# One gate group of each pair of FFN blocks in seven products of weight and token sums

## The chip, the cores and the metric

The kernel runs on one core of a Trainium2 chip. The core has a matrix engine (PE, with its weight loads listed as PEld), a vector engine (DVE), a scalar engine (ACT), a general engine (POOL) and a queue engine that issues DMAs (SP). Each works through its own list of instructions in order and waits for others by semaphores. Matmuls write to PSUM, eight banks of 128 x 512 floats; everything else lives in SBUF. The metric is the device time of one execution in microseconds (us); lower is better.

## The reference, cut to what matters

The program is one layer of a diffusion backbone: modulated attention over 256 latent tokens and 256 context tokens, then a modulated SwiGLU feed-forward part (FFN). The change lies in the FFN alone:

```python
D_MODEL = 2048
SEQ = 256
FFN_HIDDEN = -(-8 * D_MODEL // 768) * 256    # 5632

def swiglu(u, w_gate, w_up, w_down):
    return (jax.nn.silu(u @ w_gate) * (u @ w_up)) @ w_down

x = layer_norm(DN_ALPHA * x + g2 * swiglu(modulate(x, sh2, sc2), w_gate[layer], w_up[layer], w_down[layer]),
               ln2_g[layer], ln2_b[layer])
```

All of it is in float32, batch 1, depth 1.

## The kernel before, in words

**Numbers and splits.** PE multiplies in a reduced format (fp32r). So each operand is split in a high half (ACT casts it, L329) and a low half (DVE subtracts the high half from the original, L330), and one product of 128 tokens, 128 features and 512 columns is three matmuls: high by high, high token by low weight, low token by high weight (`mm3`, L338 to L341). The tokens' halves are u2h and u2l, 16 feature tiles of 128 by 256 tokens. Weights come as raw tiles of 4 feature tiles by 512 columns (1 MB, `load_raw`, L309), four raw buffers in all, and are split in two pieces of 128 x 1024 each (`split_raw`), with four buffers for high and four for low pieces. A buffer of a piece is given back when PE has done its last matmul on it.

**Blocks and groups.** The 5632 columns of gate and up are 11 blocks of 512. The 2048 features are four groups of 4 feature tiles (g = 0 to 3). A group of one block is 4 feature tiles x 2 token tiles x 3 = 24 matmuls, 12 on each piece. Because the modulation of the later features is known late, blocks 0 to 9 run in two halves: first group 0 (blocks 0 to 2) or groups 0 and 1 (blocks 3 to 9) of gate and up, whose sums are copied from PSUM to SBUF tiles named spill; later, when all features are there, the other groups. The first of these halves is the list `first_half`; between its steps stand sums for the modulation (adav), and near its end `z_part` transposes, scales and splits the last feature tiles. Block 10 runs whole.

**The second half** is the loop at L1646. For each block it runs gate's groups into two PSUM banks (one for each token tile), then up's into two others, and adds the spilled first half to each (`activate`: L1501 for gate, L1502 for up, on DVE). ACT takes Silu of gate (L1504), DVE multiplies (L1505) and transposes in 32 x 32 squares (L1515). The squares go to DRAM by eight small DMAs ("puts", L1520) and come back by two larger ones ("gets", L1525); ACT and DVE then split the result in halves hTh and hTl (`place`, L335 and L336) for the down projection. `turn()` counts the groups and lets puts, gets and places of a block follow some groups after it. Blocks 5 to 8 also carry `residual_base`, sixteen DVE instructions in all that prepare the residual in xt with LayerNorm rows loaded to a buffer called lgb.

**The order.** An earlier part of the program is placed by a planner of the kernel itself, which the change does not touch. In the FFN the instructions are written in the loops' order, and the framework's scheduler sets each engine's list from dependences, buffers and an estimate of durations, so a step can move ahead of its place in the code. What each engine then runs is fixed, in order.

## Time and profile before

| | |
|---|---|
| median of three runs | 1133.19 us (1132.01 to 1138.03) |
| the profiled execution's own time | 1132.56 us |
| its span, first to last instruction | 1130.8 us |
| mean granted clock of PE | 0.996 |
| casts of weights to high halves, L329 | 258 of 1055 ns |
| low halves of weights, L330 | 258 of 1221 ns |
| matmuls on u2h and u2l, L339 to L341 | 3 x 704 |

Durations that follow come from this one execution. In the list of groups a line's mean is the time of one instruction from its start to its end; instructions of one engine can overlap a little at their ends, and matmuls a lot, so what one costs in a row of them is read from the distance between starts.

### The profile page before, as it was taken

To read this page: it belongs to the slowest core of one execution; us is meant where nothing else is said; L and a number is where in the kernel's file an instruction comes from. 1 tells how busy PE (TensorE), PEld (TensorE's weight loads), DVE (VectorE), ACT (ScalarE), POOL (GpSimd) and SP (SyncE) were. 2 spreads that over 40 slices of the span, in tenths; PEclk is the share of its full clock that TensorE was granted. 3 is DMA by queue.
4 is the path that set the end of the run, shared out by engine and by line. 5 is a ranking of instruction groups with operands and counts; after the bars stand their busy time and mean duration, and the time that the engine had idled before them with its cause. 6 is when DMAs were issued, how large, how long until landed. Compare 5 with 4: busy or idle time off the path is not lost.

```text
span 1130.8 us, 14062 instructions
## 1 busy us (share of the span) xinstructions
PE 1109.5 (98%) x5255; PEld 891.3 (79%) x5255; DVE 844.1 (75%) x1070; ACT 550.8 (49%) x795; POOL 38.7 (3%) x82
## 2 busy tenths in 40 slices
PE   8999999999999999999999999999999999999996
PEld 6766688777887687888888888888888888888884
DVE  5763589999999798777777566776766787686576
ACT  3341554878684265444464444444444344343442
POOL 1000030110100000010000000000000000000000
PEclk9999999999999999999999999999999999999998
DMA  9999999778999768999876776777677898887541
GB/s 308 395 399 371 394 364 357 257 240 280 340 347 372 267 261 315 330 320 314 301 234 214 244 233 223 233 242 257 214 263 242 273 367 305 312 300 252 200 148 74
DMA packets 178317, 321.26 MB, mean 284 GB/s; under 512 B 8732, under 2 KB 43196, under 8 KB 175943
## 3 DMA queue, kind: packets, MB, share of 16 engines
q1 hardware_dynamic: 177528, 320.03, 81.3%
q8 instruction: 41, 0.67, 0.2%
q10 hardware_dynamic: 720, 0.33, 0.1%
q14 instruction: 28, 0.23, 0.1%
HBM read 304.07 MB, written 16.25 MB: 283 GB/s over the span
## 4 chain that ended last, share of the span: by engine, by line
PE 91%; DMA 3%; DVE 2%; ACT 2%; SPq 1%; issue 0%; POOL 0%; ACTq 0%; DVEq 0%; POOLq 0%
PE acc L339 27%; PE acc L340 27%; PE acc L341 27%; PE wk L1079 2%; PE wk L652 2%; DMA raw<-in_w_in_dram 1%; DVE lo L330 1%; PE wk L339 1%; PE wk L753 1%; PE wk L341 1%; PE wk L340 1%; SPq L567 1%; DMA raw<-in_w_ada_dram 1%; DMA raw<-in_w_gate_dram 0%; ACT hi L329 0%; DVE adav L464 0%
## 5 line engine op out<-in xcount | busy, mean ns | idle before, releaser
L330 DVE TENSOR_TENSOR lo<-raw,hi 128x1024 fp32r<-128x1024 f32 x258 | 312.3, 1221 | 165.3 <-ACT hi L329 162.9
L329 ACT CAST hi<-raw 128x1024 fp32r<-128x1024 f32 x258 | 271.1, 1055 | 322.7 <-PE acc L341 296.5
L339 PE MATMUL acc<-hi,u2h 128*128 128x512 f32 x704 | 274.6, 390 | 1.5 <-ACT u2h L1591 1.5
L340 PE MATMUL acc<-lo,u2h 128*128 128x512 f32 x704 | 274.0, 389 | 0.7 <-DVE lo L330 0.7
L341 PE MATMUL acc<-hi,u2l 128*128 128x512 f32 x704 | 274.1, 389 | 0.0
L339 PEld LDWEIGHTS acc<-hi,u2h 128*128 128x128 f32 x704 | 132.1, 188 | 29.6 <-ACT u2h L1591 2.4
L340 PEld LDWEIGHTS acc<-lo,u2h 128*128 128x128 f32 x704 | 132.2, 188 | 28.2 <-DVE lo L330 1.1
L341 PEld LDWEIGHTS acc<-hi,u2l 128*128 128x128 f32 x704 | 132.1, 188 | 28.1 <-DVE u2l L1592 0.6
L601 ACT CAST hi<-raw 128x1024 fp32r<-128x1024 f32 (+1 forms) x86 | 87.5, 1030 | 112.6 <-DMA raw<-in_w_in_dram 63.4
L339 PE MATMUL acc<-hi,hTh 128*128 128x512 f32 x344 | 133.8, 389 | 0.4 <-ACT acc L1742 0.4
L340 PE MATMUL acc<-lo,hTh 128*128 128x512 f32 x344 | 133.9, 389 | 0.0
L341 PE MATMUL acc<-hi,hTl 128*128 128x512 f32 x344 | 133.8, 389 | 0.0
L464 DVE SCALAR_TENSOR_TENSOR adav<-raw,cs,adav 128x512 f32<-128x512 f32 (+1 forms) x128 | 121.3, 948 | 9.2 <-DMA raw<-in_w_ada_dram 7.2
L604 DVE TENSOR_TENSOR lo<-raw,hi 128x1024 fp32r<-128x1024 f32 (+1 forms) x86 | 101.3, 1194 | 13.3 <-ACT hi L601 12.5
L339 PE MATMUL acc<-hi,uh 128*128 128x512 f32 x256 | 103.7, 405 | 2.3 <-ACT qacc L835 1.1
L340 PE MATMUL acc<-lo,uh 128*128 128x512 f32 x256 | 100.3, 392 | 0.5 <-DVE lo L604 0.5
L341 PE MATMUL acc<-hi,ul 128*128 128x512 f32 x256 | 100.1, 391 | 0.4 <-DVE ul L782 0.4
L339 PEld LDWEIGHTS acc<-hi,hTh 128*128 128x128 f32 x344 | 64.6, 188 | 14.2 <-ACT acc L1742 0.8
L340 PEld LDWEIGHTS acc<-lo,hTh 128*128 128x128 f32 x344 | 64.6, 188 | 13.6 <-DVE lo L330 0.2
L341 PEld LDWEIGHTS acc<-hi,hTl 128*128 128x128 f32 x344 | 64.6, 188 | 13.4
L339 PEld LDWEIGHTS acc<-hi,uh 128*128 128x128 f32 x256 | 48.1, 188 | 20.0 <-issue 5.6
L341 PEld LDWEIGHTS acc<-hi,ul 128*128 128x128 f32 x256 | 48.1, 188 | 11.1 <-DVE ul L782 0.7
(224 smaller groups left out, 1142.8 us busy)
## 6 DMA issues: line engine op xcount, KB each, us to landing
raw<-in_w_ada_dram SPq DMA_DIRECT2D x70, 1024.0 KB, 8.0
raw<-in_w_gate_dram SPq DMA_DIRECT2D x44, 1024.0 KB, 5.5
raw<-in_w_up_dram SPq DMA_DIRECT2D x44, 1024.0 KB, 5.6
raw<-in_w_down_dram SPq DMA_DIRECT2D x44, 1024.0 KB, 5.4
raw<-in_w_ada_dram SPq DMA_DIRECT2D x48, 512.0 KB, 5.9
raw<-in_w_in_dram SPq DMA_DIRECT2D x18, 1024.0 KB
raw<-in_w_out_dram SPq DMA_DIRECT2D x16, 1024.0 KB, 5.1
pd<-hx SPq DMA_DIRECT2D x64, 128.0 KB, 5.0
```

The costliest lines, as they stand in the source:

```text
L329: nc.scalar.copy(hi[:, :n], raw[:, s : s + n])
L330: nc.vector.tensor_tensor(lo[:, :n], raw[:, s : s + n], hi[:, :n].bitcast(F32), op=ALU.subtract)
L339: nc.tensor.matmul(ps, lhsT=xh, rhs=w[0], start=first, stop=False, skip_group_check=seeded)
L340: nc.tensor.matmul(ps, lhsT=xh, rhs=w[1], start=False, stop=False, skip_group_check=seeded)
L341: nc.tensor.matmul(ps, lhsT=xl, rhs=w[0], start=False, stop=last, skip_group_check=seeded)
L464: nc.vector.scalar_tensor_tensor(a[:, c : c + piece], raw[:, f : f + piece], cs[:, 4 * (g * (G4 * NB // w) + j) + 2, None], a[:, c : c + p ...
L567: nc.sync.dma_start(room.t, w[k0 * P : (k0 + 1) * P, c0 : c0 + width])
L601: nc.scalar.copy(hl.hi[:, :n], raw.t[:, s : s + n])
L604: nc.vector.tensor_tensor(hl.lo[:, :n], raw.t[:, s : s + n], hl.hi[:, :n].bitcast(F32), op=ALU.subtract)
L652: nc.tensor.matmul(bank.t[32 * j : 32 * j + 32, :width], lhsT=cs[:, 4 * k + 2 - 2 * i : 4 * k + 34 - 2 * i], rhs=raw.t[:, c * width : (c + ...
L753: nc.tensor.transpose(ps.t[:, (j * 2 + t) * P : (j * 2 + t + 1) * P], src, ident)
L1079: nc.tensor.matmul(o_ps.t[:, : 2 * P].rearrange("p (g q) -> p g q", q=32), lhsT=v, rhs=pv[:, k], start=k == 0, stop=k == 3)
```

## The change

For blocks 0 to 9, taken in pairs, the gate group g = 2 (feature tiles 8 to 11) of both blocks is no longer computed as 8 products of 128 tokens x 256 features x 512 columns but as 7, by Winograd's form of Strassen's scheme. The two token tiles by two feature halves make a 2 x 2 matrix, and two feature halves by two blocks another. `token_forms` makes the sums of tokens once, from an unsplit copy (ufs, in the buffer lgb), and splits them (fh, fl). `folded` makes four sums of raw weights in place, in the two raw tiles r1 and r2 of the pair, and runs the seven products, called here by their numbers in the code: 11, 1, 2, 12, 3, 4, 22. Each is 2 feature tiles x 3 = 6 matmuls on one piece. Partial results move between PSUM banks by three ACT copies a pair (L1534, L1542, L1550); the result of product 1 is added by DVE to the spill of the pair's second block (L1545).

Between the products stand up's groups of the two blocks: the order of a late pair is 11, a group of up, 1, a group of up, 2, 12, a group of up, 3, 4, a group of up, 22, then the other gate group of the first block and of the second. So both gate halves of a pair end behind each other, and up is done before them. From block 2 on, up's banks begin with its spilled first half, copied there by ACT (L1724), and ACT copies the finished sums back (L1730); DVE's adds for up remain in the first pair alone. Multiply and transposes of a block are now steps that follow at the next turns. The first-half step of block 3 is put ahead of z_part(4).

```diff
@@ -48,6 +48,7 @@
+FOLD_K = 8
@@ -1463,13 +1464,14 @@
-    def z_part(kk):
+    def z_part(kk, uf=None):
         ps = wk_bank()
...
-        uf = pb.tile([P, 2, SEQ], F32, tag="t2k", name="uf2", bufs=4)
+        if uf is None:
+            uf = pb.tile([P, 2, SEQ], F32, tag="t2k", name="uf2", bufs=4)
@@ -1487,22 +1489,74 @@
-    def project(accs, w_, f, g, first, last):
+    def project(accs, w_, f, g, first, last, seeded=False):
         w = load_split(w_, g * 4, f * NB)
         for j in range(4):
             k = g * 4 + j
             for t in range(NT):
-                mm3(accs[t], u2h[:, k, t * P : (t + 1) * P], u2l[:, k, t * P : (t + 1) * P], w[j], k == first, k == last)
-
-    def activate(f, t, gate, up, hh):
-
-        if f < SPLIT_F:
-            sg, su = spills[f][0][:, t, :], spills[f][1][:, t, :]
-            nc.vector.tensor_add(sg, sg, gate)
-            nc.vector.tensor_add(su, su, up)
-            gate, up = sg, su
-        nc.scalar.activation(hh, gate, AF.Silu)
-        nc.vector.tensor_mul(hh, up, hh)
+                mm3(accs[t], u2h[:, k, t * P : (t + 1) * P], u2l[:, k, t * P : (t + 1) * P], w[j],
+                    k == first and not seeded, k == last, seeded)
+    forms = {}
+    def token_forms(v):
+        v1, v2 = v[:, 0:2, :], v[:, 2:4, :]
+        a11, a21, a12, a22 = v1[:, :, :P], v1[:, :, P:], v2[:, :, :P], v2[:, :, P:]
+        tt = nc.vector.tensor_tensor
+        tt(a22, a21, a22, op=ALU.add)
+        tt(a21, a11, a21, op=ALU.subtract)
+        tt(a11, a22, a11, op=ALU.subtract)
+        tt(a12, a12, a11, op=ALU.subtract)
+        for n, (lr, x) in enumerate((((2, 3), v1), ((4, 1), v2))):
+            hi, lo = (pb.tile([P, 2, SEQ], F32R, tag="t2k", name=name, bufs=4) for name in ("fh", "fl"))
+            split(hi, lo, x)
+            for i, m in enumerate(lr):
+                forms[m] = [(hi[:, j, i * P : (i + 1) * P], lo[:, j, i * P : (i + 1) * P]) for j in range(2)]
+        for m, (t, k) in {11: (0, FOLD_K), 12: (0, FOLD_K + 2), 22: (1, FOLD_K + 2)}.items():
+            forms[m] = [tuple(u[:, k + j, t * P : (t + 1) * P] for u in (u2h, u2l)) for j in range(2)]
+    def fold_products(ps, m, piece, first):
+        w = split_raw(piece)
+        for j in range(2):
+            mm3(ps, *forms[m][j], w[j], first and j == 0, j == 1, not first)
+    def folded(w_, f, between):
+        half = 2 * NB
+        r1, r2 = (load_raw(w_, FOLD_K, G4, (f + i) * NB, NB) for i in range(2))
+        b11, b21, b12, b22 = r1[:, :half], r1[:, half:], r2[:, :half], r2[:, half:]
+        a, e = wk_bank(), wk_bank()
+        b, c, d = (acc_bank() for _ in range(3))
+        tt = nc.vector.tensor_tensor
+        fold_products(a, 11, b11, True)
+        nc.scalar.copy(b, a)
+        tt(b11, b12, b11, op=ALU.subtract)
+        between(0)
+        fold_products(e, 1, b11, True)
+        tt(b12, b22, b12, op=ALU.subtract)
+        tt(b11, b22, b11, op=ALU.subtract)
+        between(1)
+        fold_products(b, 2, b11, False)
+        nc.scalar.copy(c, b)
+        for t in range(NT):
+            sg = spills[f + 1][0][:, t, :]
+            tt(sg, sg, e, op=ALU.add)
+        fold_products(a, 12, b21, False)
+        tt(b21, b21, b11, op=ALU.subtract)
+        between(2)
+        fold_products(c, 3, b12, False)
+        nc.scalar.copy(d, c)
+        fold_products(b, 4, b22, False)
+        between(3)
+        fold_products(c, 22, b21, False)
+        return (a, c), (b, d)
+    def gated_half(f, t, gate):
+        hh = spills[f][0][:, t, :]
+        nc.vector.tensor_add(hh, hh, gate)
+        nc.scalar.activation(hh, hh, AF.Silu)
@@ -1538,9 +1592,17 @@
             hh, hx = ([c[:, t, :] for t in range(NT)] for c in spills[f])
         else:
             hh, hx = ([t2k(name) for t in range(NT)] for name in ("hh", "hx"))
-        for t in range(NT):
-            activate(f, t, gu[0][t], gu[1][t], hh[t])
+        def gated(t):
+            if f >= SPLIT_F:
+                nc.scalar.activation(hh[t], gu[0][t], AF.Silu)
+            nc.vector.tensor_mul(hh[t], gu[1][t], hh[t])
             squares(hh[t], hx[t])
+        late = 1 if f < SPLIT_F else 0
+        if not late:
+            for t in range(NT):
+                gated(t)
         hd, hf = {}, {}
         def puts():
@@ -1556,7 +1618,7 @@
             for t in range(NT):
                 place(f, t, hf[t])
-        return [[PUT, puts], [GET, gets], [PLACE, places]]
+        return [[1 + t, lambda t=t: gated(t)] for t in range(NT * late)] + [[2 * late + n, step] for n, step in ((PUT, puts), (GET, gets), (PLACE, places))]
@@ -1626,12 +1688,15 @@
     run(first_half[2:3])
     run(merge(first_half[3 : 2 * ONE_F], scales))
     combine(1)
+    run(first_half[2 * ONE_F : 2 * ONE_F + 1])
     z_part(4)
     z_part(6)
     cutoff = len(first_half) - 2
-    run(merge(first_half[2 * ONE_F : cutoff], side))
-    for kk in range(EARLY_G * 4, KD, 2):
-        z_part(kk)
+    run(merge(first_half[2 * ONE_F + 1 : cutoff], side))
+    ufs = pb.tile([P, 4, SEQ], F32, tag="lgb", name="ufs")
+    for i, kk in enumerate(range(EARLY_G * 4, KD, 2)):
+        z_part(kk, ufs[:, 2 * i : 2 * i + 2, :] if kk < FOLD_K + 4 else None)
+    token_forms(ufs)
     run(first_half[cutoff:])
     flips = []
@@ -1643,9 +1708,47 @@
             flips.remove(e)
             e[1]()
-    for f in range(FFN // NB):
-        if 5 <= f < 9:
-            residual_base(f - 5)
+    for f0 in range(0, SPLIT_F, 2):
+        for f in (f0, f0 + 1):
+            if 5 <= f < 9:
+                residual_base(f - 5)
+        ups = {}
+        def up(i, g):
+            f = f0 + i
+            su = [spills[f][1][:, t, :] for t in range(NT)]
+            if g == groups[f]:
+                ups[i] = [wk_bank() for _ in range(NT)]
+                for t in range(NT):
+                    if f0:
+                        nc.scalar.copy(ups[i][t], su[t])
+            project(ups[i], w_up, f, g, groups[f] * 4, KD - 1, f0 > 0)
+            turn()
+            if g == ng - 1:
+                for t in range(NT):
+                    if f0:
+                        nc.scalar.copy(su[t], ups[i][t])
+                    else:
+                        nc.vector.tensor_add(su[t], su[t], ups[i][t])
+        def between(n):
+            i, last = divmod(n, 2)
+            gs = range(groups[f0 + i], ng)
+            for g in gs[-1:] if last else gs[:-1]:
+                up(i, g)
+        gates = folded(w_gate, f0, between)
+        for i, f in enumerate((f0, f0 + 1)):
+            for g in range(groups[f], ng):
+                if g * 4 != FOLD_K:
+                    project(gates[i], w_gate, f, g, None, KD - 1, True)
+                    turn()
+            for t in range(NT):
+                gated_half(f, t, gates[i][t])
+            turn()
+            flips += flip_steps(f, (None, [spills[f][1][:, t, :] for t in range(NT)]))
+    for f in range(SPLIT_F, FFN // NB):
         gu = []
         for w_ in (w_gate, w_up):
             accs = [acc_bank() for _ in range(NT)]
```

Three places show how the engines' lists move. A number behind a name tells one tile from another.

DVE, at the end of a gate half late in the stage: before, the adds for gate of block 6 (spill_3712) and what surrounds them.

```order
L330 TENSOR_TENSOR lo_6494<-raw_6487,hi_6493 128x1024
L330 TENSOR_TENSOR lo_6524<-raw_6521,hi_6523 128x1024
L1501 TENSOR_TENSOR spill_3712<-spill_3712,acc_6399 128x512
L1501 TENSOR_TENSOR spill_3712<-spill_3712,acc_6400 128x512
L330 TENSOR_TENSOR lo_6528<-raw_6521,hi_6527 128x1024
L330 TENSOR_TENSOR lo_6579<-raw_6576,hi_6578 128x1024
L330 TENSOR_TENSOR lo_6583<-raw_6576,hi_6582 128x1024
```

DVE, now: the same adds for block 6 (spill_3712) and block 7 (spill_3714); lo_6834 and lo_6892 are low halves for products 11 and 1 of the next pair, whose raw tiles are raw_6824 and raw_6826.

```order
L331 TENSOR_TENSOR lo_6834<-raw_6824,hi_6833 128x1024
L1558 TENSOR_TENSOR spill_3712<-spill_3712,wk_6465 128x512
L1558 TENSOR_TENSOR spill_3712<-spill_3712,acc_6468 128x512
L1535 TENSOR_TENSOR raw_6824<-raw_6826,raw_6824 128x1024
L1599 TENSOR_TENSOR spill_3712<-spill_3713,spill_3712 128x512 x2
L1569 STREAM_TRANSPOSE spill_3713<-spill_3712 128x4x4x32 x2
L331 TENSOR_TENSOR lo_6852<-raw_6849,hi_6851 128x1024
L1558 TENSOR_TENSOR spill_3714<-spill_3714,acc_6467 128x512
L1558 TENSOR_TENSOR spill_3714<-spill_3714,acc_6469 128x512
L331 TENSOR_TENSOR lo_6856<-raw_6849,hi_6855 128x1024
L1599 TENSOR_TENSOR spill_3714<-spill_3715,spill_3714 128x512
L1538 TENSOR_TENSOR raw_6826<-raw_6826 128x1024
```

Before, two adds stand between low halves; now the adds, multiplies and transposes of two blocks and two sums of weights stand between the low halves of two up pieces. The next rows are a transpose, lo_6892, the low half of a piece of up, the third sum of weights, another low half, a multiply, and the low half for product 2.

ACT, where up changes from the first block of a pair to the second (blocks 4 and 5); wk_6120 is a bank of the first, wk_6240 and wk_6241 are the second's. Before, this engine has only casts, Silus and places there.

```order
L330 CAST hi_6229<-raw_6099 128x1024
L336 CAST hTh_6520<-spill_3704 128x4x128
L330 CAST hi_6246<-raw_6244 128x1024
L1730 COPY spill_3709<-wk_6120 128x512
L1724 COPY wk_6240<-spill_3711 128x512
L1730 COPY spill_3709<-wk_6121 128x512
L1724 COPY wk_6241<-spill_3711 128x512
L330 CAST hi_6250<-raw_6244 128x1024
L1542 COPY acc_6106<-acc_6105 128x512
L330 CAST hi_6278<-raw_6101 128x1024
```

Four copies of up, a place that needs a get, and a copy between banks now stand among the casts.

SP, in the pair of blocks 6 and 7: raw_6608 and raw_6669 are the third and fourth load of up, hd is the DRAM buffer of the puts and gets of blocks 4 (spill_3709, spill_3708) and 5.

```order
L310 DMA raw_6540<-in_w_up_dram 128x4x512
L1579 DMA spill_3706<-hd_6435 128x512
L1579 DMA spill_3706<-hd_6440 128x512
L1574 DMA hd_6753<-spill_3709 32x4x128 x4
L1574 DMA hd_6758<-spill_3709 32x4x128 x2
L310 DMA raw_6608<-in_w_up_dram 128x4x512
L1574 DMA hd_6758<-spill_3709 32x4x128 x2
L1579 DMA spill_3708<-hd_6753 128x512
L1574 DMA hd_6805<-spill_3711 32x4x128
L310 DMA raw_6669<-in_w_up_dram 128x4x512
```

Before, in the same place for block 4 (gate loads raw_6441, up loads raw_6487 and raw_6521):

```order
L1520 DMA hd_6475<-spill_3709 32x4x128 x3
L309 DMA raw_6441<-in_w_gate_dram 128x4x512
L1520 DMA hd_6475<-spill_3709 32x4x128
L1520 DMA hd_6480<-spill_3709 32x4x128 x4
L309 DMA raw_6487<-in_w_up_dram 128x4x512
```

Before, two up loads follow a block's eight puts and are ahead of its gets; now the third load of up stands behind six puts, and the fourth behind nine puts and a get.

## The prediction

> **What bounds the kernel now.** I read the page first: busy shares and the chain of work that ended last.
>
> ```profile
> span 1130.8 us, 14062 instructions
> ...
> PE 1109.5 (98%) x5255; PEld 891.3 (79%) x5255; DVE 844.1 (75%) x1070; ACT 550.8 (49%) x795; POOL 38.7 (3%) x82
> ...
> PE 91%; DMA 3%; DVE 2%; ACT 2%; SPq 1%; issue 0%; POOL 0%; ACTq 0%; DVEq 0%; POOLq 0%
> ```
>
> PE is busy 98% of the span and is 91% of that chain. A share of the whole span says little about one stage, so next come windows inside the stage that the change rewrites, the second half of blocks 0 to 9 (about 580 to 835 us).
>
> ```profile
> core 0: us, PE busy (x) PEld busy (x) DVE busy (x) ACT busy (x) POOL busy (x), PEclk, DMA share, GB/s
> ...
> 700.00:752.00 52.00, 52.00 (x231) 43.04 (x230) 38.03 (x46) 25.23 (x29) 0.00 (x0) 1.00 0.72 233
> 752.00:804.00 52.00, 52.00 (x231) 43.07 (x230) 37.80 (x44) 25.25 (x29) 0.00 (x0) 1.00 0.77 251
> ```
>
> PE has no gap at a granted clock of 1.00; DVE is busy 38.03 of 52 us (73%), ACT 25.23 (49%). A busy PE row hides its pace, since ends overlap, so I take the pace from starts in the timeline.
>
> ```profile
> 624.78 0.39 PE L339 MATMUL acc<-hi,u2h 128*128 128x512 f32 x1
> 624.98 1.05 ACT L329 CAST hi<-raw 128x1024 fp32r<-128x1024 f32 x1 [1.67 <-PE acc L341]
> 625.00 0.39 PE L340 MATMUL acc<-lo,u2h 128*128 128x512 f32 x1
> 625.01 0.19 PEld L341 LDWEIGHTS acc<-hi,u2l 128*128 128x128 f32 x1
> ...
> 641.10 0.39 PE L339 MATMUL acc<-hi,u2h 128*128 128x512 f32 x1
> ```
>
> Between the first and the last row lie 72 matmuls: 16.32 / 72 = 0.2267 us each. A piece (half a raw tile, 12 matmuls) is 2.72 us, a group 5.44, one folded product (6 matmuls) 1.36. The ACT row shows the latency I use below: the cast waits for a PE piece that ends as the first row's matmul starts, and begins 0.20 us later. The list of PE's waits, cut to 540 to 900 us, is empty; the longest of the whole span is elsewhere.
>
> ```profile
> PE acc L339 <- ACT u2h L1591: 1.5, 1, 1.5
> ```
>
> So PE's instruction count sets the time here, as long as both halves of each piece arrive in time.
>
> **The matmuls removed.** One gate group of two blocks is 2 blocks x 4 feature tiles x 2 token tiles x 3 = 48 matmuls; seven folded products are 7 x 2 x 3 = 42. Six fewer in each of five pairs: 30 x 0.2267 = **6.8 us**, all on the path.
>
> [...]
>
> **DVE.** Its back-to-back costs come from starts in its timeline.
>
> ```profile
> 702.27 1.23 DVE L330 TENSOR_TENSOR lo<-raw,hi 128x1024 fp32r<-128x1024 f32 x1 [1.49 <-ACT hi L329]
> 703.41 1.28 DVE L1502 TENSOR_TENSOR spill<-spill,acc 128x512 f32<-128x512 f32 x2
> 704.61 1.29 DVE L1505 TENSOR_TENSOR spill<-spill 128x512 f32<-128x512 f32 x2
> 705.81 1.30 DVE L1515 STREAM_TRANSPOSE spill<-spill 128x512 f32<-128x512 f32 x2
> 707.03 2.32 DVE L330 TENSOR_TENSOR lo<-raw,hi 128x1024 fp32r<-128x1024 f32 x2
> ```
>
> A low half takes 1.14 us until the next instruction starts (1.23 to its own end); adds, multiplies and transposes of 512 take 0.60 to 0.61. No sum of raw weights is in this trace; the low half has the same shape, two SBUF inputs and an SBUF result, so I take 1.14 (bounds: the 0.60 of half the width, and 1.23). A late pair (blocks 4 to 9, two groups left of each pass) costs now 16 low halves and 20 small ones, 18.2 + 12.1 = 30.3 of 43.5 us. Changed: 19 low halves, 4 weight sums, 18 small ones (two adds of the shared product come, four adds of up go): 26.2 + 10.9 = 37.1 of 42.2 us, **88%**. DVE stays under PE, but in order, so bursts matter more than the total. The worst burst is the seam of two pairs, where both gate halves end 5.44 us apart instead of 21.76. Let PE finish the first gate half at 0; it then runs the second's group (to 5.44), product 11 (6.80), an up group (12.24), product 1 (13.60), an up group (19.04), products 2 and 12 (20.40, 21.76). By the order shown above, DVE does two adds, a weight sum, two multiplies, two transposes, a low half, two adds, a low half, a multiply, a weight sum, a transpose, then the low half of product 1: 1.20 + 1.14 + 1.20 + 1.22 + 1.14 + 1.20 + 1.14 + 0.60 + 1.14 + 0.61 + 1.14 = 11.73. From 0.20, and 0.09 more to the end of the last, that is 12.02; PE's first matmul on it is at 12.24 and the second, which reads the low half, at 12.47. From there to the low half of product 12 are 8.11 us more (four low halves, a weight sum, a multiply, a transpose, two adds): 20.13 against 20.40 to 20.63. So PE waits for nothing, by 0.2 to 0.5 us. Three seams are that tight (before blocks 4, 6, 8); before block 2 the gate halves end 10.88 us apart, and before block 10 no weight sums follow. Behind a late low half stand the following ones, so a lateness is paid once per seam, and the middle of the pair gives it back. The adds are a wait for PE in DVE's queue with all this behind them, but DVE reaches the second two at 6.10, after the half ended at 5.44.
>
> **ACT.** Now in a 52 us window it works 25.23.
>
> ```profile
> L1576 ACT COPY spill<-acc x36: 582/589/590, 410.9 to 584.2; 128x512 f32<-128x512 f32 x36
> ...
> L1742 ACT COPY acc<-xt x2: 586/588/591, 1102.6 to 1106.8; 128x512 f32<-128x512 f32 x2
> ```
>
> Each pair adds three casts of 1.05, three copies from bank to bank (not in the trace; between nothing and the two rows' 0.59 and 0.59 added, taken as 0.59), and from block 2 on eight copies of up: 3.2 + 1.8 + 4.7 = 9.7 us, on some 21 of 42. They lie beside PE. The copy that waits for product 11 (7.0) has the cast of product 1's weights behind it; ACT reaches it at 8.0, after the Silus. The tightest is the turn from one up to the next: PE needs the new seed 2.72 us after the last matmul of the old; the first copy out can start 0.5 us before that (t = 0 ends three matmuls earlier, plus 0.20), four copies at 0.59 end at 1.9, the second seed 1.5 us before its use. A cast queued ahead uses 1.05 of this.
>
> **DMA and SP's queue.** The fold holds two of four raw buffers; up's loads turn in the other two.
>
> ```profile
> raw<-in_w_up_dram SPq DMA_DIRECT2D x44, 1024.0 KB, 5.6
> ...
> hd<-spill SPq DMA_DIRECT2D x80, 64.0 KB, 4.6
> spill<-hd SPq DMA_DIRECT2D x20, 256.0 KB, 5.4
> ```
>
> The third up load can go out when the low half of the first is done (8.44 on the clock above), and lands at 14.0; its cast cannot start before 16.5, when PE gives a hi buffer back, and need not before 19.4. In SP's order it stands behind six puts that need the transposes of 4.96, so they pass first. The get of the finished block follows: puts out by 6.2, landed 10.8, get landed 16.2, and the ACT cast that waits for it (ahead of the next up cast) is reached at 16.4. All is covered, by 2 to 5 us.
>
> **The beginning.** The token sums (four DVE instructions of 256 columns, not in the trace; between the 0.16 us of the four-column copy below and 0.60; 0.35 lies halfway) and two splits add 2.6 us to DVE and 1.2 to ACT before product 1 needs them; the sixteen residual instructions (L1487, L1488, 0.60 each back to back, 9.8 us) move from there into the first pair. That pair's 282 matmuls last 63.9 us, and DVE's work in them is 31 x 1.14 + 22 x 0.605 + 9.8 = 58.5, with no seam before it.
>
> ```profile
> 565.88 0.16 DVE L1164 COPY sh<-wk 128x4 f32<-128x4 f32 x1 [0.62 <-PE wk L1157]
> ...
> 590.11 1.29 DVE L1487 SCALAR_TENSOR_TENSOR xt<-xt,lgb 128x512 f32<-128x512 f32 x2 [0.90 <-DMA lgb<-in_ln_g_dram]
> ...
> 548.00:580.00 32.00, 32.00 (x157) 26.47 (x156) 22.95 (x27) 19.64 (x29) 0.55 (x3) 1.00 0.77 260
> ```
>
> The last row is the window: nine us of DVE are free there. I cost it at nothing; if that cover failed, PE would wait up to the 2.6 us, once.
>
> **Sum.** The profiled execution took 1132.56 us (0.6 below the median of 1133.19; span 1130.8 plus 1.8 around it). 1132.6 - 6.8, and 0.8 for waits of about 0.2 at four seams, which I allow since the margins of 0.2 are smaller than what I can read: **1126.6 us**.
>
> **The rivals.** *The seams cost more.* If each of the fourteen instructions before product 1's low half took its stand-alone time (0.09 more for the four long ones, 0.08 for the ten short, by the ends in the rows above), DVE would be 1.2 us later and PE would wait 0.7 to 0.9, and about the same again at product 12: with four seams 3 to 8 us, 1129 to 1134. For it: margins of 0.2 to 0.5; waits for ACT in between. Against: DVE runs back to back in every such burst above. Centre 1131.
>
> *A matmul gives back less than the pace.* If it gave back only what its weight load takes, 0.19 us in the row above, the saving would be 5.7 us: 1127.7. Against it: each load lies beside the matmul ahead of it, and the pace is that of the matmuls.
>
> [...]
>
> *Slower: loads late in the fold.* Two raw buffers, in a queue with puts that wait for DVE and gets that wait for puts. If a transpose comes late, the put holds up the third up load. PE waits once the load lands 5.4 us late (19.4 against 14.0). To be slower by over 0.5% each of four pairs must lose (5.7 + 6.8) / 4 = 3.1 us, a load 8.5 us late: 1139 to 1148, centre 1142. For it: SP now waits long for puts.
>
> ```profile
> SPq L309 <- DVE lo L330: 115.1, 39, 7.6
> SPq L1520 <- DVE spill L1515: 48.1, 9, 5.4
> ```
>
> Against: the longest wait of a put is 5.4 us, and in the new order the transposes come early. [...]
>
> **How the numbers follow.** Forecast (waits of 0 to 2.5 us, 1125.8 to 1128.3) 0.52; seams 0.24; less per matmul 0.04; slower 0.14; something better, under 1125.5, 0.06. The range 1125 to 1134 holds these but the last two, 0.80. A measurement of this kernel tells 0.5% (5.7 us) from no change, so faster means under 1127.5: four fifths of the forecast and the better case, 0.42 + 0.06 = 0.48. Same: the rest of it, seams and less per matmul, 0.38. Slower 0.14.
>
> **What would show it.** In the changed profile: 30 fewer matmuls at 0.2267 us; PE's waits in the stage under 1 us in total, if any on low halves of products 1 and 12; DVE near 88% in the late pairs; raw loads landing in 5 to 6 us. PE waits on low halves at each seam of a microsecond or more say the second case; PE or ACT waiting for raw loads or for gets, the slower one; a pace other than 0.2267, the third. I am wrong altogether if ACT's in-order copies, which I followed at one turn only, hold PE.

## The result, and the profile after

| | before | changed |
|---|---|---|
| median | 1133.19 us (7 runs, 1131.44 to 1138.03) | 1128.06 us (7 runs, 1127.31 to 1130.85) |
| ratio, with its 95% interval | | 0.9954 (0.9936 to 0.9973) |
| the profiled execution and its span | 1132.56, 1130.8 us | 1130.85, 1129.1 us |

The change makes the kernel 5.1 us faster. The forecast was 1126.6, so 1.5 us are missing. Of these, 0.6 are the forecast's starting point alone, which was the profiled 1132.56 and not the median of 1133.19; the rest is looked for here. The profiled execution happens to be the slowest of the seven. The page of the changed kernel:

```profile
span 1129.1 us, 14104 instructions
...
PE 1104.7 (98%) x5225; PEld 884.8 (78%) x5225; DVE 880.7 (78%) x1105; ACT 589.1 (52%) x859; POOL 35.1 (3%) x82
...
L330 ACT CAST hi<-raw 128x1024 fp32r<-128x1024 f32 x273 | 284.7, 1054 | 272.2 <-PE acc L342 212.3
L331 DVE TENSOR_TENSOR lo<-raw,hi 128x1024 fp32r<-128x1024 f32 x273 | 328.9, 1219 | 117.6 <-ACT hi L330 113.4
```

PE has its 30 matmuls less (5255 to 5225), DVE and ACT their 15 splits more (258 to 273 low and high halves). Next the two windows of 42.2 us that hold late pairs (busy time of each engine):

```profile
core 0: us, PE busy (x) PEld busy (x) DVE busy (x) ACT busy (x) POOL busy (x), PEclk, DMA share, GB/s
690.00:732.20 42.20, 42.20 (x187) 34.94 (x187) 36.49 (x40) 26.35 (x34) 0.00 (x0) 1.00 0.67 213
732.20:774.40 42.20, 42.20 (x188) 34.92 (x187) 37.28 (x42) 29.08 (x38) 0.00 (x0) 1.00 0.76 249
```

DVE works 36.5 and 37.3 us where 37.1 were worked out, and PE has no gap. The waits of the stage (560 to 880 us; total, times, longest), which was empty for PE before, now read:

```profile
ACT hi L330 <- DMA raw<-in_w_up_dram: 4.3, 2, 2.3
...
DVE xt L1489 <- DMA lgb<-in_ln_g_dram: 3.2, 1, 3.2
ACT hTh L336 <- DMA spill<-hd: 3.1, 2, 1.7
PE wk L340 <- ACT wk L1724: 2.9, 2, 2.3
```

PE's waits are not on a low half, where the prediction put them, but on ACT's copy of up's spill into its bank (L1724). The timeline shows the longer one, at the seam before block 2, the first with seeded banks. DVE first:

```profile
638.99 1.29 DVE L1489 SCALAR_TENSOR_TENSOR xt<-xt,lgb 128x512 f32<-128x512 f32 x2 [3.21 <-DMA lgb<-in_ln_g_dram]
640.20 1.22 DVE L331 TENSOR_TENSOR lo<-raw,hi 128x1024 fp32r<-128x1024 f32 x1
641.34 0.68 DVE L1558 TENSOR_TENSOR spill<-spill,wk 128x512 f32<-128x512 f32 x1
...
651.81 1.27 DVE L1558 TENSOR_TENSOR spill<-spill,acc 128x512 f32<-128x512 f32 x2
```

then ACT and PE:

```profile
648.08 0.59 ACT L1724 COPY wk<-spill 128x512 f32<-128x512 f32 x1
652.52 1.23 ACT L1559 ACTIVATE spill<-spill 128x512 f32<-128x512 f32 x2 [3.85 <-DVE spill L1558]
653.65 0.58 ACT L1534 COPY acc<-wk 128x512 f32<-128x512 f32 x1
654.17 0.58 ACT L1724 COPY wk<-spill 128x512 f32<-128x512 f32 x1
...
654.80 0.50 PE L340 MATMUL wk<-hi,u2h 128*128 128x512 f32 x1 [2.32 <-ACT wk L1724]
```

It is a chain through three engines. The last residual instruction of the first pair waits 3.21 us for its broadcast vector (buffer lgb), and everything in DVE's list behind it, which from there runs without a gap, is late, among it the adds of block 1's gate half at 651.81. ACT's Silu waits for these, and the seed of the second token tile stands behind the Silu in ACT's list. So PE waits 2.32 us for a copy that has nothing to do with the residual.

To compare runs I take the "FFN part": from the start of the first to the start of the last matmul on u2h. What lies before it varies from run to run (the first of these matmuls starts between 391.2 and 393.9 us in the fourteen profiles of this study) and would hide one microsecond. Rows of before, in the list of instructions by tile (durations, first and last start):

```profile
L339 PE MATMUL acc<-hi,u2h x704: 387/389/504, 391.9 to 877.1; 128*128 128x512 f32 x176
L340 PE MATMUL acc<-lo,u2h x704: 389/389/500, 392.2 to 877.3; 128*128 128x512 f32 x176
```

and of the changed kernel:

```profile
L340 PE MATMUL acc<-hi,u2h x422: 389/389/504, 393.6 to 875.4; 128*128 128x512 f32 x141
L341 PE MATMUL acc<-lo,u2h x422: 387/389/402, 393.9 to 875.7; 128*128 128x512 f32 x141
```

877.3 - 391.9 = 485.4 us before, 875.7 - 393.6 = 482.1 after: a gain of 3.3, which is 6.8 for the matmuls less 2.9 of waits and 0.6 that the list of waits does not have. The spans differ by 1.7 only, since in this execution the FFN part starts 1.7 us later.

### The profile page after: what moved, and what is told of

Read it like the earlier page. It is cut to its first block, busy times and chain, and to the rows that moved or that the text cites. A ratio compares the mean times of both kernels' runs of the same rounds, so it can differ in the third digit from the quotient of the medians.

```text
span 1129.1 us, 14104 instructions
## 1 busy us (share of the span) xinstructions
PE 1104.7 (98%) x5225; PEld 884.8 (78%) x5225; DVE 880.7 (78%) x1105; ACT 589.1 (52%) x859; POOL 35.1 (3%) x82
## 4 chain that ended last, share of the span: by engine, by line
PE 86%; DMA 6%; DVE 3%; ACT 3%; SPq 1%; issue 1%; ACTq 0%; DVEq 0%
PE acc L340 22%; PE acc L342 22%; PE acc L341 22%; PE wk L340 5%; PE wk L342 5%; PE wk L341 5%; DMA raw<-in_w_in_dram 3%; PE wk L1080 2%; PE wk L653 1%; DVE lo L331 1%; DMA raw<-in_w_out_dram 1%; DMA lgb<-in_ln_g_dram 1%; DMA spill<-hd 1%; DMA pd<-hx 1%; SPq L568 1%
## 5 line engine op out<-in xcount | busy, mean ns | idle before, releaser
L331 DVE TENSOR_TENSOR lo<-raw,hi 128x1024 fp32r<-128x1024 f32 x273 | 328.9, 1219 | 117.6 <-ACT hi L330 113.4
L340 PE MATMUL acc<-hi,u2h 128*128 128x512 f32 x422 | 165.0, 391 | 2.0 <-ACT u2h L1653 1.5
L341 PE MATMUL acc<-lo,u2h 128*128 128x512 f32 x422 | 164.3, 389 | 0.0
L342 PE MATMUL acc<-hi,u2l 128*128 128x512 f32 x422 | 164.1, 390 | 0.0
L340 PEld LDWEIGHTS acc<-hi,u2h 128*128 128x128 f32 x422 | 79.1, 188 | 19.4 <-ACT u2h L1653 2.4
L340 PE MATMUL wk<-hi,u2h 128*128 128x512 f32 x232 | 90.5, 390 | 2.9 <-ACT wk L1724 2.9
L342 PEld LDWEIGHTS acc<-hi,u2l 128*128 128x128 f32 x422 | 79.2, 188 | 17.3 <-DVE u2l L1654 0.6
L341 PEld LDWEIGHTS acc<-lo,u2h 128*128 128x128 f32 x422 | 79.2, 188 | 16.2
L342 PE MATMUL wk<-hi,u2l 128*128 128x512 f32 x232 | 90.3, 389 | 0.0
L341 PE MATMUL wk<-lo,u2h 128*128 128x512 f32 x232 | 90.3, 389 | 0.0
```

The lines of the kernel that those rows point to most:

```text
L331: nc.vector.tensor_tensor(lo[:, :n], raw[:, s : s + n], hi[:, :n].bitcast(F32), op=ALU.subtract)
L340: nc.tensor.matmul(ps, lhsT=xh, rhs=w[0], start=first, stop=False, skip_group_check=seeded)
L341: nc.tensor.matmul(ps, lhsT=xh, rhs=w[1], start=False, stop=False, skip_group_check=seeded)
L342: nc.tensor.matmul(ps, lhsT=xl, rhs=w[0], start=False, stop=last, skip_group_check=seeded)
```

## The experiments

The experiments weigh three theories. Theory A: PE's matmuls set the time and give back their 6.8 us whole; what is missing is the chain above. Theory B: the added work on DVE, the weight sums above all, uses up its room at the seams. Theory C: ACT's order alone, the seed behind the Silu, makes the wait.

| run | median, us | ratio to before (95%) | FFN part, us | PE's longest wait in the FFN part past 425 us, us |
|---|---|---|---|---|
| loads by POOL | 1127.61 | 0.9944 (0.9932 to 0.9956) | 478.6 | 0.5 |
| early seed | 1127.03 | 0.9942 (0.9929 to 0.9955) | 480.2 | 1.3, low half |
| product 22 twice | 1132.94 | 0.9996 (0.9988 to 1.0005) | 485.4 | 0.5 |
| POOL, no sums | 1131.68 | 0.9987 (0.9979 to 0.9995) | 483.3 | 1.8, low half |
| changed kernel again | 1128.24 | 0.9954 (0.9942 to 0.9966) | 479.2 | 0.5 |
| residual late | 1135.42 | 1.0017 (1.0008 to 1.0025) | 486.9 | 2.4, low half |
| no residual, no sums | 1126.98 | 0.9942 (0.9929 to 0.9955) | 478.8 | 0.5 |
| residual late, up by DVE | 1136.57 | 1.0027 (1.0016 to 1.0037) | 489.3 | 4.4, DVE's gate add |
| half the residual early | 1136.60 | 1.0029 (1.0018 to 1.0040) | 489.1 | 7.9, u2l |
| POOL, two sums more | 1130.37 | 0.9971 (0.9960 to 0.9982) | 483.0 | 2.4, low half |
| POOL, up by DVE | 1127.51 | 0.9942 (0.9930 to 0.9955) | 479.4 | 0.5 |
| residual on POOL | 1127.52 | 0.9946 (0.9934 to 0.9958) | 480.5 | 1.3, low half |

Each ratio is to runs of the kernel before that were taken beside it (medians 1133.2 to 1133.7). The 0.5 is a wait near 436 us on u2h, which all the changed versions have (1.2 with half the residual early); before has one of 0.7 there on a low half.

**Loads by POOL.**

```diff
-        nc.sync.dma_start(lg, ln1_g[0:1, sl].to_broadcast([P, NB]))
-        nc.sync.dma_start(lb, ln1_b[0:1, sl].to_broadcast([P, NB]))
+        nc.gpsimd.dma_start(lg, ln1_g[0:1, sl].to_broadcast([P, NB]))
+        nc.gpsimd.dma_start(lb, ln1_b[0:1, sl].to_broadcast([P, NB]))
```

> The two loads of the residual base (L1486, L1487) are issued by POOL in place of SP, nothing else in the source differs. Theory A (TensorE's matmuls set the time; what is missing of the 6.8 us is one wait, 2.32 us at 654.80, and its cause is the load that SP issues behind five gate loads): the 3.2 us of VectorE behind lgb goes, and with it the wait of the first matmuls of block 2's up group; the span falls by 1.5 to 2.5, the time to 1125.5 to 1126.8. Theory B (VectorE's added work, the weight sums above all, fills its slack at the seams): VectorE does the same work, so the wait stays at 1.5 or more, somewhere in the first two pairs; 1127.5 to 1129. Theory C (ScalarE's list alone puts the seed of token tile 1 behind block 1's Silus, whatever VectorE does): the gate half still ends where TensorE lets it, and 0.5 to 1.5 of the wait stays; about 1127 to 1128.

PE waits for nothing in the stage.

```profile
L340 PE MATMUL acc<-hi,u2h x422: 389/389/504, 392.2 to 870.6; 128*128 128x512 f32 x141
L341 PE MATMUL acc<-lo,u2h x422: 387/389/402, 392.5 to 870.8; 128*128 128x512 f32 x141
```

The FFN part is 870.8 - 392.2 = 478.6 us, and 485.4 - 478.6 = 6.8 us shorter than before: the whole of the matmuls' term. ACT's list changed with it (both seeds ahead of the second Silus), so this run alone does not part A from C. DVE still waits for vectors; they come at places where it has time:

```profile
DVE xt L1489 <- DMA lgb<-in_ln_g_dram: 3.7, 2, 2.3
```

The median, 1127.61, is only 0.5 below the changed kernel's. It lies above the 1126.8 that theory A allowed and in the ranges of B and C, so it is the profile that speaks for A here, and not the time.

**Early seed.** The residual's loads stay with SP; the next pair's first up banks are seeded ahead of block 1's gate halves.

```diff
...
+            if i and f + 1 < SPLIT_F:
+                early[0] = up_banks(f + 1)
...
```

> The next pair's first up banks are taken and seeded right behind the up groups of the pair before, ahead of block 1's gate halves in the source, so that ScalarE seeds both ahead of its Silus; the residual's loads stay on SP. Theory A: VectorE still waits 3 us for lgb, but no matmul stands behind that any more; the 2.32 us goes, and so does most of the 0.56 us at 791.65; 1125.3 to 1126.8. Theory B: the wait only moves to the next low half that VectorE is late with (product 11's or product 1's of pair 1), 1.5 us or more on another row; 1127.5 to 1129. Theory C: the same as theory A. All three fail if the two banks, held earlier, make another group wait for a bank: then a new wait of TensorE on ACT's L1737 or DVE's L1558 rows, and 1128 or more.

DVE still stood still for the vector in the first pair, yet no matmul waited there:

```profile
637.62 1.29 DVE L1489 SCALAR_TENSOR_TENSOR xt<-xt,lgb 128x512 f32<-128x512 f32 x2 [2.56 <-DMA lgb<-in_ln_g_dram]
```

So at this seam the lateness of DVE reaches PE only through the seed behind the Silu. In this run PE waits 1.3 us for a low half at 796.25 instead, in the up group behind product 1 of the last pair. Theory B had a wait on a low half, but in the second pair, and the median, 1127.03, lies between the ranges of A and B.

**Product 22 twice.**

```diff
-        fold_products(c, 22, b21, False)
+        w = split_raw(b21)
+        for n in range(2):
+            for j in range(2):
+                mm3(c, *forms[22][j], w[j], False, n == 1 and j == 1, True)
```

> Product 22's six matmuls are issued a second time, from a second split of the same weights, so that each pair has the 48 matmuls of before and everything else of the change; product 22 is counted twice in the output. Theory A: 30 matmuls by 0.2267 us are 6.8 us on TensorE, whole: 1134.0 to 1136.0, and the wait at the first seam stays. If the removed matmuls had been hiding behind something else (theory B in its strong form, VectorE or the loads set the pace of the folded stage), the 30 come at less than half their price: below 1131.5. The second split adds five hi and five lo of 1.05 and 1.22 us, so theory B weakly adds another 1 to 3 us on top: above 1136.5.

```profile
L340 PE MATMUL acc<-hi,u2h x432: 389/389/504, 392.3 to 877.5; 128*128 128x512 f32 x144
L341 PE MATMUL acc<-lo,u2h x432: 387/389/397, 392.7 to 877.7; 128*128 128x512 f32 x144
```

The FFN part is 877.7 - 392.3 = 485.4 us, that of before to the tenth, with everything else of the change in place. The median is a microsecond below what A gave: the wait at the first seam, which A had staying, is not in this profile. 30 matmuls are 6.8 us, taken away or put back.

**POOL, no sums.** As the first, without the lines of the four weight sums.

> The residual's loads by POOL as in the first run, and the four weight sums of each pair left out (products 1, 2, 3 and 22 then use weights that are not summed, so the output differs from the reference's): 20 instructions by 1.14 to 1.22 us, 22.8 to 24.4 us less on VectorE. Theory A: nothing on TensorE waits for a sum, so it stands within 0.7 us of the first run. Theory B: it is faster than the first run by 1.0 us or more. Theory C: no difference from the first run.

All three theories missed: 24 us less work on DVE, and 4 us slower. The scheduler gave DVE another order, in which a residual instruction stands ahead of a low half of the up group behind product 12:

```profile
603.16 1.22 DVE L331 TENSOR_TENSOR lo<-raw,hi 128x1024 fp32r<-128x1024 f32 x1
606.07 0.69 DVE L1489 SCALAR_TENSOR_TENSOR xt<-xt,lgb 128x512 f32<-128x512 f32 x1 [1.70 <-DMA lgb<-in_ln_g_dram]
606.68 1.22 DVE L331 TENSOR_TENSOR lo<-raw,hi 128x1024 fp32r<-128x1024 f32 x1
```

PE waits 1.84 us for that low half, and then its clock is at 0.50 for 3.41 us (last section). This speaks for A in a wider form: what costs is a residual instruction that waits for its vector, where something that PE needs soon stands behind it in DVE's list. Whether DVE's load costs anything by itself, the run without residual and sums tells.

**The changed kernel again.**

> The changed kernel itself once more, beside the others on this chip. From the first lot, the part from the first to the last FFN matmul that reads u2h took 482.06 us with the change, 478.61 where POOL loads the residual's vectors, 485.42 before. Theory A (6.8 us come from 30 matmuls whole, and one wait at the seam before block 2 gives a part back in each run, by when the residual's load lands): median 1127.5 to 1128.7, and the profiled run shows again a wait of TensorE of 1 to 3 us behind ACT's L1724 near 654. If the wait is of the one profiled run only (it was the slowest of 7), no such row, and the median is 1126.5 to 1127.5.

PE has no wait near 654, but the same chain stands there with other numbers, which makes it a natural experiment:

```profile
637.04 1.29 DVE L1489 SCALAR_TENSOR_TENSOR xt<-xt,lgb 128x512 f32<-128x512 f32 x2 [0.88 <-DMA lgb<-in_ln_g_dram]
...
649.86 1.28 DVE L1558 TENSOR_TENSOR spill<-spill,acc 128x512 f32<-128x512 f32 x2
...
652.22 0.58 ACT L1724 COPY wk<-spill 128x512 f32<-128x512 f32 x1
...
652.85 0.50 PE L340 MATMUL wk<-hi,u2h 128*128 128x512 f32 x1
```

The vector's load is issued 0.37 us later than in the first profile (631.21, against 630.84), but it lands after 5.8 us instead of 8.2; DVE waits 0.88 us instead of 3.21, and PE starts at 652.85, within 0.2 of its turn. The list of instructions is the same: between these two executions, the landing time of one 256 KB load decides how much the chain costs. The median came out as theory A said, the profile as its opponent.

This execution's own time, 1128.25, is that of the median, and its FFN part is short:

```profile
L340 PE MATMUL acc<-hi,u2h x422: 389/389/504, 393.9 to 872.8; 128*128 128x512 f32 x141
L341 PE MATMUL acc<-lo,u2h x422: 387/389/398, 394.3 to 873.1; 128*128 128x512 f32 x141
```

It is 873.1 - 393.9 = 479.2 us, 6.2 shorter than before, but it starts 2.0 us later (393.9 against 391.9). So what this execution lacks is lost ahead of the FFN part and not in the chain. What the executions without a profile lost, and where, cannot be read.

**Residual late.** The vectors take buffers that are free only behind the last product.

```diff
-        lgb = pb.tile([P, 2, NB], F32, tag="lgb", name="lgb")
-        lg, lb = lgb[:, 0, :], lgb[:, 1, :]
+        lg, lb = (pb.tile([P, NB], F32, tag="t2k", name=name, bufs=4) for name in ("lg", "lb"))
```

> The residual base takes its two vectors from buffers that the folded stage's token halves hold until product 22 of the last pair, so its loads and its 16 VectorE instructions come after the last product, where VectorE has room; output as the reference's. Theory A: no instruction behind lgb stands in VectorE's list of the first pair any more, and ScalarE seeds both banks ahead of block 1's Silus; no wait of TensorE over 0.4 us between 560 and 820; the part from the first to the last such matmul 478.5 to 479.5, the time 1125.3 to 1126.8. Theory B (VectorE is full at each seam, and any seam may be late): the seams before blocks 4, 6 and 8 keep 1 us or more in sum, 1127 to 1129.

The first seam is free of waits, as A said, but all sixteen instructions now come together, and low halves of the last groups stand behind them:

```profile
PE acc L341 <- DVE lo L331: 3.1, 2, 2.4
PE wk L341 <- DVE lo L331: 1.6, 1, 1.6
```

My expectation that DVE has room there was wrong: it counted busy time.

**No residual, no sums.** Both are left out, so nothing of DVE's list waits for a vector.

> The residual base and the four weight sums of each pair are left out (the output lacks the first, and products 1, 2, 3 and 22 use weights that are not summed). The first lot's run without sums was slower than the one with them, since two residual instructions behind lgb then stood ahead of product 1's low half, and TensorE's wait of 1.84 us was followed by 3.4 us at half the granted clock. Theory A: with nothing behind lgb, leaving out 24 us of VectorE's work gains nothing: within 0.8 us of the run with the residual late, no wait over 0.4 us, no stretch at half clock. Theory B: faster than that run by 1 us or more. If the sums' absence as such costs time (other data in the products, another order), it is slower by 2 us or more, as in the first lot.

The FFN part is 478.8 us, against 478.6 with the sums and the loads by POOL. Leaving out 24 us of weight sums and 10 us of residual gains nothing: theory B falls. (The expectation has two residual instructions ahead of product 1's low half in the run without sums; that run's rows show one, ahead of a low half of an up group.) The run named for comparison, the residual late, turned out to have waits of its own, so the run with the loads by POOL takes its place.

**Up added by DVE,** with the residual late and with the loads by POOL.

```diff
-                    if f0:
-                        nc.scalar.copy(ups[i][t], su[t])
-            project(ups[i], w_up, f, g, groups[f] * 4, KD - 1, f0 > 0)
+                    pass
+            project(ups[i], w_up, f, g, groups[f] * 4, KD - 1)
...
-                    if f0:
-                        nc.scalar.copy(su[t], ups[i][t])
-                    else:
-                        nc.vector.tensor_add(su[t], su[t], ups[i][t])
+                    nc.vector.tensor_add(su[t], su[t], ups[i][t])
```

> The residual late as above, and up not seeded: VectorE adds up's spill to the banks as before the change (16 more instructions of 0.68 us, 10.9 us, on VectorE, and 32 copies of 0.59 us less on ScalarE). Theory A: TensorE's matmuls are the same, and the first up matmuls wait for no copy; within 0.8 us of the run with the residual late, unless VectorE passes its room: 2.7 us more in each late pair of 42.2 us, by the prediction's walk 39.8 of 42.2. Theory B: VectorE is late at the seams, 0.5 to 1.5 us at each of four, so 2 to 6 us slower than the run with the residual late, with rows of TensorE on DVE's L331 or L1729.

> The residual's loads by POOL, and up not seeded: VectorE adds up's spill to the banks in every pair, as before the change (16 instructions of 0.68 us more on VectorE, 32 copies of 0.59 us fewer on ScalarE). It tells what the seeding earns by itself, apart from the residual's place. Theory A: TensorE's matmuls are the same; VectorE has the room for 2.7 us a pair; within 0.8 us of the run with the loads by POOL (1127.6, ratio 0.9944). The prediction's walk (37.1 of 42.2 us taken, 39.8 with this): 0.5 to 1.5 us at each of four seams, 2 to 6 us slower than that run, with rows of TensorE on DVE's L331 or L1727.

The first is 1.2 us slower than the run with the residual late, outside the 0.8 that theory A allowed, but by waits that all lie past 820 us, where the late residual stands; at the four seams PE waits for nothing. The second is level with the loads by POOL (479.4 and 478.6; ratios 0.9942 and 0.9944). Seeding up in PSUM earns nothing that can be measured here, and DVE carries 2.7 us more in each late pair with no wait of PE.

**Half the residual early.** Slices 0 and 1 right behind z_part(6), loads by POOL.

> Two of the residual's four slices (n = 0 and 1, whose columns have been transposed by z_part(6)) are worked right there, ahead of the token forms, and the loads of all four are issued by POOL; output as the reference's. So 8 of the 16 VectorE instructions leave the folded stage for the first half of the FFN, where VectorE is about 0.77 busy. Theory A (6.8 us of matmuls whole, and a wait of 0 to 3 us that varies from run to run with the landing of the residual's vectors, in whose place VectorE's list stands still): no wait of TensorE over 0.4 us between 560 and 880, 478.5 to 479.2 us from the first to the last matmul that reads u2h, median 1125.8 to 1127.2 and no run over 1128.5. If the eight instructions now hold VectorE in the first half, a new wait on DVE's lo rows between 440 and 500 and 1127.5 or more.

This is the clearest case of the mechanism, and theory A's forecast for it was missed by 9 us: the first load is issued at 423.70, and DVE stands still from 426.4 to 430.9.

```profile
430.91 0.69 DVE L1489 SCALAR_TENSOR_TENSOR xt<-xt,lgb 128x512 f32<-128x512 f32 x1 [4.55 <-DMA lgb<-in_ln_g_dram]
...
440.46 1.29 DVE L1489 SCALAR_TENSOR_TENSOR xt<-xt,lgb 128x512 f32<-128x512 f32 x2 [0.85 <-DMA lgb<-in_ln_g_dram]
442.88 0.69 DVE L1490 SCALAR_TENSOR_TENSOR xt<-lgb,xt 128x512 f32<-128x512 f32 x1 [1.12 <-DMA lgb<-in_ln_b_dram]
443.49 0.69 DVE L1479 TENSOR_TENSOR u2l<-uf,u2h 128x512 fp32r<-128x512 f32 x1
```

Behind these is a low half of tokens (u2l), for which PE waits 7.9 us.

**POOL, two sums more.**

```diff
         tt(b11, b22, b11, op=ALU.subtract)
+        tt(b11, b11, b11, op=ALU.max)
...
         tt(b21, b21, b11, op=ALU.subtract)
+        tt(b21, b21, b21, op=ALU.max)
```

> The residual's loads by POOL, and behind two of each pair's weight sums (L1539 and L1547) one more instruction of the same kind and size on the same piece, a maximum of the piece with itself, so the output is the reference's: 10 by 1.14 us on VectorE, 2.28 us in each pair, ahead of the splits of products 2 and 22. The prediction put the low halves of products 1 and 12 of a late pair 0.2 to 0.5 us ahead of their need at the seams. If that walk is right, 2.28 us more cannot be hidden: 1 to 2 us of new waits at each of the four late seams or within the pairs, 4 to 8 us in all, 1131 to 1136, and a wait that long may halve the clock for 3.4 us as well. Theory A: no wait on VectorE was seen at those seams, so the room is wider than the walk said; 0 to 1.5 us in all, 1126.5 to 1129.

It is 3 us slower than without (ratios 0.9971 and 0.9944), which is more than theory A said, though not where the prediction's walk put it: all its waits are in the first pair, and from block 2 on PE waits for nothing.

```profile
603.96 0.69 DVE L1489 SCALAR_TENSOR_TENSOR xt<-xt,lgb 128x512 f32<-128x512 f32 x1 [1.86 <-DMA lgb<-in_ln_g_dram]
604.57 1.22 DVE L1548 TENSOR_TENSOR raw<-raw 128x1024 f32<-128x1024 f32 x1
605.71 1.28 DVE L1734 TENSOR_TENSOR spill<-spill,wk 128x512 f32<-128x512 f32 x2
606.90 1.22 DVE L1549 TENSOR_TENSOR raw<-raw 128x1024 f32<-128x1024 f32 x1
608.04 4.62 DVE L331 TENSOR_TENSOR lo<-raw,hi 128x1024 fp32r<-128x1024 f32 x4
```

The residual's 1.86 us and the added 1.14 (L1549) stand ahead of one low half, and PE waits 2.37 us for it.

**Residual on POOL.** Loads and arithmetic, the constant first multiplied into the vectors.

```diff
...
-            nc.vector.scalar_tensor_tensor(xt[:, t, sl], xt[:, t, sl], ALPHA, lg, op0=ALU.mult, op1=ALU.mult)
-            nc.vector.scalar_tensor_tensor(xt[:, t, sl], lb, ALPHA, xt[:, t, sl], op0=ALU.mult, op1=ALU.add)
+            nc.gpsimd.tensor_mul(xt[:, t, sl], xt[:, t, sl], lg)
+            nc.gpsimd.tensor_add(xt[:, t, sl], xt[:, t, sl], lb)
```

> The residual base as a whole is moved to POOL, which does nothing else from 590 to 850: its loads, and three operations a slice in place of VectorE's two (a scaling of both vectors by the constant, then a product and a sum per token tile); output as the reference's. VectorE loses 16 instructions of 0.68 us and, more to the point, no instruction in its list waits for lgb any more. Theory A: whatever the landing of the vectors, no split stands behind it; no wait of TensorE over 0.4 us between 560 and 880, 478.5 to 479.3 us from the first to the last matmul that reads u2h, median 1125.8 to 1127.3, no stretch at half the clock, and less scatter than the changed kernel (1127.1 to 1130.9). Against it: if POOL's rows (a 128x128 product took it 0.95 us) slow VectorE's beside them, the lo rows go above 1.3 us in those stretches and waits on DVE's L331 come back; 1127.5 or more.

No row of DVE behind lgb is left. The other case came true instead: beside POOL's rows DVE's go from 1.22 to 2.30 us (last section), and PE waits 1.31 us for such a low half at 655.24. No version tried is clearly faster than 0.9942, and that is about what 6.8 of 1133.2 us come to (0.9940).

## Why the prediction was right, and where it was not

**The matmuls removed: right.** They are worth 6.8 us, shown twice in the FFN part: 485.4 before, 478.6 without the 30 where nothing waits, 485.4 with the 30 put back. This also rejects the rival of a smaller gain per matmul.

**DVE's sums: right in size.** 36.5 and 37.3 us of 42.2 in late pairs, against 37.1. The token sums took 0.42 each, not 0.35.

**The allowance for waits: too small in one profile, enough in the other.** The sum had 0.8 us at four seams. The first profile has 2.9 us of waits, and all of them on ACT's copies; the second has none past 560 us, and its FFN part of 479.2 us is 485.4 - 6.8 + 0.6. The three seams called tight did not show the waits on low halves that the walk feared. One reason can be read before block 6, in the second profile of the changed kernel: the first gate add starts at 739.74 and product 1's first matmul at 752.49, 12.75 us apart where the walk had 12.04 (12.24 - 0.20). Token tile 0's bank ends three matmuls, 0.68 us, before the other, and its add can start then. The seam before block 2, called loose, has the wait of 2.32 us, and only a bank seeded by ACT carries it. "I am wrong altogether if ACT's in-order copies, which I followed at one turn only, hold PE" named the right place without a price, and by that sign the first profile is against the prediction and the second is not. The other 0.56 us lie before block 8; ahead of the copies there ACT waits 2.3 us for an up load and 1.7 for a get, so the cover of 2 to 5 us that the prediction gave the transfers was not there in that execution.

**The residual "at nothing": what the first profile shows to be wrong.** It was costed by DVE's busy time, 58.5 of 63.9 us (in the first profile 52.7 in the 63.9 us from product 11 on, so there was room), and with no seam before the pair. But the pair has a seam behind it, and the last of these sixteen instructions wait for a load that starts only when one buffer comes free, and then behind five gate loads in SP's queue. The price is not their 9.8 us but the time DVE's list stands still, less what the seam has to spare: of 3.21 us PE waited 2.32, of 0.88 us nothing that is listed. In before the same instructions ran at 571 to 606 us, and PE waited for none. The fallback of 2.6 us, once, is near the 2.32 by luck: it was the length of the token sums and their splits, which no matmul waited for.

**The time: within the forecast's own range, in part by luck.** The median of 1128.06 lies in the forecast's own 1125.8 to 1128.3, but above the 1127.5 that the prediction set for faster, so it is the case "same", to which it gave 0.38 against 0.48. The starting point was 0.6 us below before's median, and the start of the FFN part alone moves by 2.7 us from profile to profile, more than the forecast's miss.

**The rivals.** Seams cost more: not by DVE's load, which is rejected by the run without residual and sums. Slower by late raw loads: ACT waited for them (2.3 us at most), and PE waited at most the 0.56 us behind it. Stretches at about half the clock stand in four of the experiments (matmul starts 0.43 us apart), and none in the FFN part of the changed kernel's two profiles (no matmul on u2h over 0.51 us long there, against 0.63 to 0.80).

**What stays open.** The medians of the changed kernel (1128.1 and 1128.2) and of the run with the loads by POOL (1127.6) differ by less than their intervals, so the times alone do not show the wait. That the chain costs what is missing in the median is not shown: of two profiles, whose FFN parts are 3.5 and 0.6 us above the shortest, the one with the median's time has almost none of it and starts its FFN part late. Why the start moves was not looked into. Theory C is not excluded as a part: the seed behind the Silu is a condition of the wait at this seam, and the late vector is what fills it.

## What to carry to other kernels

In these runs an instruction that waits for a load cost what its engine's list stood still, less what there was to spare, whatever its own length: in the first profile DVE stood still for 3.21 us ahead of two instructions that took 1.29, and PE waited 2.32. It cost more where half the clock followed (3.41 us at 0.50 in the run without sums). So when a change moves such instructions, ask where their loads are issued and what stands behind them, and not if the engine has room. Count what hangs on the copy that seeds a bank, too: it tied a matrix product to what its engine waited for (ACT 3.85 us for DVE, PE 2.32 us for ACT). And a wait that depended on one transfer's landing differed between two executions of the same list: 8.2 us to land and 2.32 us of waiting in one, 5.8 us and no listed wait in the other.

## What the runs showed of the hardware

**Some waits of PE were followed by half its clock, others were not.** The run without sums in two windows (start and end, length, PE's busy time and matmuls, its clock with 1.00 for full speed, then what the DMAs did):

```profile
605.34:608.75 3.41, 1.57 (x7) 1.00 0.28 78
608.75:612.16 3.41, 3.41 (x9) 0.50 0.07 13
```

PE waits for 1.84 us in the first window, and in the second has half the clock: matmuls start 0.427 us apart instead of 0.227, eight in 3.41 us where 15 fit (the row counts those that overlap its ends as well). In the run with two sums more, PE waited longer (2.37 us, and 0.24 just before) and kept its clock:

```profile
604.59:608.01 3.42, 2.12 (x9) 1.00 0.00 0
608.01:611.42 3.41, 2.11 (x9) 1.00 0.02 5
611.42:614.83 3.41, 3.41 (x17) 1.00 0.92 298
```

It also stayed at 1.00 behind the 2.32 us of the changed kernel's first profile (652 to 658.4 us). In three other runs matmuls started 0.43 us apart for a while behind a long wait: of 2.43 us with the residual late, of 4.43 with up added by DVE besides, and of 7.85 with half the residual early, where the clock was 0.53 from 444.2 to 447.6 us. So the length of the wait alone does not tell the two kinds apart: half the clock followed 1.84 us, and did not follow 2.32 or 2.37. What decides is not shown.

**DVE was slower beside POOL.** Low halves and weight sums take 1.22 us on DVE; in the run with the residual on POOL, beside POOL's rows, they take up to 2.30 (and POOL's own products and sums 1.97 and 2.15 us each on average):

```profile
645.22 4.43 POOL L1490 TENSOR_TENSOR xt<-xt,lgb 128x512 f32<-128x512 f32 x2
648.42 2.30 DVE L1536 TENSOR_TENSOR raw<-raw 128x1024 f32<-128x1024 f32 x1
649.60 4.50 POOL L1491 TENSOR_TENSOR xt<-xt,lgb 128x512 f32<-128x512 f32 x2
...
652.88 2.30 DVE L331 TENSOR_TENSOR lo<-raw,hi 128x1024 fp32r<-128x1024 f32 x1
```

Why they were slower is not shown.
